# Quarter sums of the MLP's second weight: from accumulating transfers to VectorE, and another order of the mixed products behind them

## The chip, the cores and the metric

The kernel runs on one core of a Trainium2 chip. The metric is the device time of one execution in microseconds (us). A core has five instruction streams that matter here: TensorE (PE), VectorE (DVE), ScalarE (ACT), GpSimd (POOL) and SyncE (SP). Each works through its own stream in order. In this kernel POOL and SP issue transfers and do no arithmetic; a transfer is named here by the queue that issues it.

## What is computed

One layer of a decoder on a sequence of 2048 rows and 1024 channels, all in fp32:

```python
h = x * (1 + sc1) + sh1
z = h @ w_in                       # 1024 -> 2048: gates B and C, values v (3 x 512), pool (512)
y_conv = B * short_conv(C * v)     # causal, width 3
y_pool = multi_scale_pool(pool)    # windows 2, 4, 8, 16, a 128x128 map per window
x = layer_norm(ALPHA * x + (1 + g1) * (concat(y_conv, y_pool) @ w_out))
h = x * (1 + sc2) + sh2
f = square(relu(h @ w_mlp_in)) @ w_mlp_out        # 1024 -> 4096 -> 1024
x = layer_norm(ALPHA * x + (1 + g2) * f)
```

The shifts, scales and gates come from a conditioning vector c through a linear map.

## The kernel before

**Products.** Every fp32 matrix is held as a high part and a low part (`split`, L80 to L82: ScalarE casts the high part at L81, VectorE subtracts it at L82 and gets the low part). A product is three matmuls, high by high, high by low, low by high (`mm3`, L85 to L88). Large products are done by the Strassen-Winograd scheme, seven half-size products in place of eight, in the order

```python
ORDER = (("11", "11"), ("12", "21"), ("s2", "2"), ("s1", "1"), ("s3", "3"), ("s4", "22"), ("22", "4"))
```

The first name is the left operand (a block, or a sum s1 to s4 of blocks), the second the right one (a block, or a weight sum 1 to 4). "s1 by 1" is the fourth of these, "12 by 21" the second.

**Stages.** The sequence is worked in two blocks of 1024 rows (b = 0 and 1). Each goes through the input projection, the output projection with the first layer norm, the MLP's first product (up) in 8 groups of 512 hidden channels, and its second product (down) with the second layer norm. All buffers are in pools: o (12 tiles of 128x1024), h (28), w (6), r (5), and PSUM (8 banks).

**Input projection of block 1** (`in_proj_1`, L616). Four groups j, interleaved. At the end of a group other than the last, `store_mixed` (L340) sends the group's results and their Strassen sums to `msum` in DRAM by four transfers on POOL's queue; the output projection loads them back as r tiles (r<-msum). In the same queue, behind these stores, stand calls of `sum_quarters`.

**Quarter sums.** In block 1, three of down's seven products are themselves done by the Strassen scheme on quarters of 256 columns. Their right operands are sums of quarters of the weights, `wquart`, for n = 0, 1, 2 (product 12 by 21 is n = 0, s4 by 22 is n = 1, s1 by 1 is n = 2). `sum_quarters(n, step)` (L993) makes them with transfers alone, DRAM to DRAM, 512 KB each: step 0 copies (L1001), steps 1 to 3 add into what was copied (L998). There are 24 copies and 24 accumulating transfers, all on POOL's queue. The table `SUM_TURNS` (L717) puts most of them behind the input projection's groups; three more calls stand in the output projection (L935, L936, L945).

**Output projection** (`out_proj`, L852). `load_x` (L859) loads a tile of 128 rows of x, also on POOL's queue: four tiles ahead of the first product, four ahead of product 3. Products accumulate into four PSUM banks X and four banks Y, which is all eight. `begin` (L877) is a VectorE instruction, ALPHA times x plus a bank, which frees nothing until x is there; `end` (L881) adds a further bank.

**Up** (`up`, L1006). A group is 7 products of 24 matmuls of 128x512. Its results are stored as usum by POOL; in block 1 three of them go as quarters, with their sums, to `uquart` (`save_quarters`, L968). In block 0 the same loop also makes the sums of the weights for down, `w2sum`, by `sum_blocks` (L951): loads of 256 KB on SP, four VectorE adds of 128x512, four stores on POOL, at the end of a group.

**Down of block 1** (`down`, L1116). The first 37 units are mixed by the string `MIX`: a "1" is a unit "c", one group of a whole product (product 0, then product 2: 8 units of 24 matmuls of 128x512 each), a "0" a unit "f", one of the seven quarter products of a product k in the order of `FINE` (1, 5, 3), 48 matmuls of 128x256. An f unit reads uquart and wquart (L1140 to L1145). Its bank is evicted by ScalarE (`fine_copy`, L1173) or VectorE (`fine_add`, `fine_less`, `fine_from`, L1177 to L1185), in pieces of 128x256 into the result tiles F. Product 0 stays in PSUM, and VectorE adds it to F (L1286 to L1288) after the last quarter product of k = 1.

Of the kernel before, what the change touches and what calls it, by code (L numbers as in the profile page):

```python
# [11 lines left out]
ALU = mybir.AluOpType  # L12
# [20 lines left out]
WW = T + HALO  # L33
MIX = "1110101010101000100100100101001001001"

# [8 lines left out]
def tile_hybrid_layer(ctx: ExitStack, tc: tile.TileContext, opening, xT, x, wada, vec, win0, win,  # L44
# [295 lines left out]
    def store_mixed(j, y, pt, u, v):  # L340
        for i, r in ((0, y), (2, pt), (4, u[:, :T])):
            nc.gpsimd.dma_start(msum[i : i + 2, j].rearrange("a p n -> p a n"),
                                r.rearrange("p (a n) -> p a n", a=2))
        return nc.gpsimd.dma_start(msum[6, j], v[:, :H]).ins

# [270 lines left out]
    def in_proj_1(X, W, first_w):  # L616
# [14 lines left out]
        def group(j):  # L631
# [58 lines left out]
            if last:  # L690
                mixed[1] = sums[0]
                mixed.extend(sums[1:])
            else:
                done = store_mixed(j, y, pt, u, v)
            with nullcontext() if last else tc.issue_after(done):
                for n, step in SUM_TURNS[j]:
                    sum_quarters(n, step)

# [15 lines left out]


    SUM_TURNS = (((0, 0),), ((1, 0), (0, 1)), ((2, 0), (1, 1), (0, 2)), ((2, 1), (1, 2), (0, 3)))

# [134 lines left out]
    def out_proj(b, ops):  # L852
# [80 lines left out]
        ops.whole(5)  # L933
        if b:
            sum_quarters(2, 2)  # L935
            sum_quarters(1, 3)  # L936
        matmuls(4, Y, False, every, first_row)
# [5 lines left out]
        back(0)  # L943
        if b:
            sum_quarters(2, 3)  # L945
        matmuls(6, X, False, every, last_row)
# [40 lines left out]

    def quarter_sum(n, hf, i):
        return wquart[n, hf, i].rearrange("p (g n) -> p g n", n=Q)

    SUM_STEPS = (((0, 1), (2, 1), (1, 3), (3, 2)), ((0, 0), (2, 3)), ((1, "0"),), ((3, "1"),))

    def sum_quarters(n, step):  # L993
        for hf in range(2):
            for i, what in SUM_STEPS[step]:
                src = quarter_sum(n, hf, int(what)) if what in ("0", "1") else weight_quarter(n, what, hf)
                if step:
                    nc.gpsimd.dma_start(quarter_sum(n, hf, i), src, accum_op=ALU.add,  # L998
                                        max_dma_last_dim=4096)
                else:  # L1000
                    nc.gpsimd.dma_start(quarter_sum(n, hf, i), src)  # L1001

# [113 lines left out]
    def down(b, F, g2, close):  # L1116
# [3 lines left out]
        if b:  # L1120
            parts_ = [("f", k, m) for k in FINE for m in range(7)]
            groups = [("c", i, g) for i in (0, 2) for g in range(NC)]
# [64 lines left out]
        def fine_product(i, m, ops):  # L1187
            bank = {0: "x", 1: "y", 2: "x", 3: "z", 4: "x", 5: "z", 6: "x"}[m]
            new = m in (0, 1, 3)
            if new:  # L1190
                fine_banks[bank] = t_ps()
            ps = fine_banks[bank]
            fine_matmuls(ps, ops, new)
            how, row, col = {0: (fine_copy, 0, 0), 1: (fine_add, 0, 0), 2: (fine_copy, 0, 1),
                             3: (fine_copy, 1, 1), 4: (fine_less, 1, 1), 5: (fine_from, 0, 1),
# [72 lines left out]
        if b:  # L1268
            table[0] = X, True, lambda t, ps: None
            table[2] = X, False, first_row  # L1270
# [4 lines left out]
        for n, (kind, i, part_) in enumerate(units):  # L1275
# [8 lines left out]
            if kind == "f":  # L1284
                fine_product(i, part_, ops)
                if (i, part_) == (1, 6):  # L1286
                    for t in range(4):
                        add(t, lo_, X[t])  # L1288
                if (i, part_) == (3, 6):
                    for t in range(4):  # L1290
# [105 lines left out]
    def mlp(b, B, back, g2):  # L1396
# [9 lines left out]
        if b == 0:  # L1406
            for g in range(NC):
                sums += [(sum_blocks, w2[g], w2sum[g], p) for p in halves]
                if g == 3:
                    sums += [(sum_weights, wins[0], winsum, p) for p in halves]  # L1410

        for g in range(NC):
            for _ in ups[g]:
                pass
            for make, src, dst, p in sums[: HALF_SUMS[g]]:
                make(src, dst, t_o, which=[p])
            del sums[: HALF_SUMS[g]]
# [71 lines left out]
```

## Time and profile before

| | |
|---|---|
| time, 3 runs | 1799.73, 1800.35, 1802.71 us (median 1800.35) |
| profiled execution | 1806.26 us |
| its span in the trace | 1804.5 us |
| mean granted TensorE clock | 0.984 |
| busy: TensorE, VectorE, ScalarE, POOL | 1735.6, 1330.3, 890.4, 276.5 us |
| moved by transfers | 514.04 MB, 285 GB/s |

How to read it. Busy times are those of one profiled execution, and the span is the time from its first to its last instruction. A row of a window gives its start and end, its length, the busy time of an engine with the count of its instructions, then the clock that TensorE was granted (1.00 is full), the busy share of the DMA engines and what they moved in GB/s. A row of the waits names the waiting engine and line, behind the arrow the engine and line that ended the wait, then the total, the number of waits and the longest. In a row of a timeline the brackets hold the idle time before the instruction and what ended it. L878 is line 878 of the kernel before.

### The profile page before, as it was taken

The page shows a single profiled execution, that of the slowest core. Times are in us where ns is not written, and L with a number is a line of the kernel's source. Part 1 is how long each engine was busy: PE and PEld are TensorE (multiplying, and loading weights), DVE is VectorE, ACT ScalarE, POOL GpSimd, SP SyncE. Part 2 cuts the span into 40 slices and gives each one's busy share as a digit, 9 for nine tenths or more (in the row PEclk, how much of TensorE's full clock was granted, in tenths as well). Part 3 has the DMA queues.
Part 4 walks back from the last instruction along what each step waited for, and adds up shares of the span by engine and source line. Part 5 has one row for each costly group of instructions (what it writes and reads, how often), then busy time and mean ns, then how long its engine had stood idle before and what let it go on. Part 6 is the DMA issues. An engine that isn't in the chain of part 4 may idle for free.

```text
span 1804.5 us, 22616 instructions
## 1 busy us (share of the span) xinstructions
PE 1735.6 (96%) x8132; PEld 1452.8 (81%) x8132; DVE 1330.3 (74%) x1756; ACT 890.4 (49%) x1202; POOL 276.5 (15%) x493
## 2 busy tenths in 40 slices
PE   9999999999999999999999983999999998999997
PEld 7888888888888888888788762788888887899986
DVE  7897788876777866687766762688766766997675
ACT  5322467544456544454743330685454455675552
POOL 0222120232222000001001322102221112100000
PEclk9999999999999999999999986999999999999999
DMA  9899766788878998789645899766554469999884
GB/s 385 324 346 336 293 238 247 292 316 319 332 296 326 417 349 308 278 315 362 223 150 192 264 284 245 230 229 222 210 205 171 154 222 388 419 391 325 292 319 180
DMA packets 158304, 514.04 MB, mean 285 GB/s; under 512 B 18288, under 2 KB 23920, under 8 KB 157936
## 3 DMA queue, kind: packets, MB, share of 16 engines
q1 hardware_dynamic: 102960, 315.97, 48.0%
q0 software_dynamic: 55232, 196.64, 30.6%
q8 instruction: 63, 1.03, 0.2%
q14 instruction: 49, 0.40, 0.1%
HBM read 359.97 MB, written 177.73 MB: 298 GB/s over the span
## 4 chain that ended last, share of the span: by engine, by line
PE 80%; DMA 8%; DVE 5%; issue 4%; ACT 2%; POOL 1%; SPq 0%; DVEq 0%; POOLq 0%; ACTq 0%
PE ps L87 24%; PE ps L86 24%; PE ps L88 23%; PE ps L1163 6%; PE ps L403 3%; DMA wquart<-in_w2q 2%; DVE h L82 1%; DVE o L91 1%; DMA o<-in_x 1%; PE ps L759 1%; DMA r<-msum 1%; DMA r<-in_xT 1%; DVE o L1365 1%; DVE o L1359 1%; ACT h L81 0%
## 5 line engine op out<-in xcount | busy, mean ns | idle before, releaser
L86 PE MATMUL ps<-h,w 128*128 128x512 f32 x1312 | 511.5, 390 | 8.2 <-DVE o L91 3.0
L88 PE MATMUL ps<-h,w 128*128 128x512 f32 x1312 | 511.9, 390 | 2.6 <-DVE w L82 2.6
L87 PE MATMUL ps<-h,w 128*128 128x512 f32 x1312 | 511.5, 390 | 0.0
L86 PE MATMUL ps<-h,h 128*128 128x512 f32 x928 | 364.0, 393 | 36.6 <-DVE o L878 30.7
L81 ACT CAST h<-r 128x1024 fp32r<-128x1024 f32 (+1 forms) x202 | 205.8, 1021 | 339.5 <-PE ps L87 117.2
L87 PE MATMUL ps<-h,h 128*128 128x512 f32 x928 | 363.5, 392 | 0.3 <-DMA h<-wlow 0.2
L88 PE MATMUL ps<-h,h 128*128 128x512 f32 x928 | 363.3, 391 | 0.0
L82 DVE TENSOR_TENSOR h<-r,h 128x1024 fp32r<-128x1024 f32 (+1 forms) x202 | 238.3, 1184 | 130.7 <-ACT h L81 129.8
L81 ACT CAST w<-r 128x1024 fp32r<-128x1024 f32 x156 | 164.3, 1053 | 271.6 <-PE ps L87 260.6
L86 PEld LDWEIGHTS ps<-h,w 128*128 128x128 f32 x1312 | 246.9, 188 | 61.3 <-DVE o L91 3.4
L88 PEld LDWEIGHTS ps<-h,w 128*128 128x128 f32 x1312 | 247.1, 188 | 55.0 <-DVE w L82 3.7
L87 PEld LDWEIGHTS ps<-h,w 128*128 128x128 f32 x1312 | 246.9, 188 | 51.8 <-DVE h L82 0.5
L82 DVE TENSOR_TENSOR w<-r,w 128x1024 fp32r<-128x1024 f32 x156 | 190.6, 1222 | 122.8 <-ACT w L81 121.5
L86 PEld LDWEIGHTS ps<-h,h 128*128 128x128 f32 x928 | 175.6, 189 | 75.4 <-DVE o L878 30.2
L87 PEld LDWEIGHTS ps<-h,h 128*128 128x128 f32 x928 | 175.7, 189 | 36.9 <-DMA h<-wlow 1.2
L88 PEld LDWEIGHTS ps<-h,h 128*128 128x128 f32 x928 | 175.4, 189 | 36.4
L91 DVE TENSOR_TENSOR o<-o,o 128x1024 f32<-128x1024 f32 (+2 forms) x222 | 183.3, 836 | 24.1 <-DMA usum<-o 17.8
L91 DVE TENSOR_TENSOR o<-o,ps 128x512 f32<-128x512 f32 (+1 forms) x168 | 110.2, 663 | 54.4 <-PE ps L88 54.0
L82 DVE TENSOR_TENSOR h<-w,h 128x1024 fp32r<-128x1024 f32 x114 | 138.9, 1218 | 10.4 <-ACT h L81 10.2
L1163 PE MATMUL ps<-h,h 128*128 128x256 f32 x1008 | 125.1, 285 | 7.1 <-ACT h L81 3.7
L1163 PEld LDWEIGHTS ps<-h,h 128*128 128x128 f32 x1008 | 124.2, 194 | 8.7 <-ACT h L81 6.5
L81 ACT CAST h<-w 128x1024 fp32r<-128x1024 f32 x114 | 119.7, 1050 | 17.4 <-DMA w<-w2sum 7.2
(158 smaller groups left out, 1444.8 us busy)
## 6 DMA issues: line engine op xcount, KB each, us to landing
usum<-o POOLq DMA_DIRECT2D x88, 512.0 KB, 3.8
r<-usum SPq DMA_DIRECT2D x88, 512.0 KB, 6.8
w<-w2sum SPq DMA_DIRECT2D x62, 512.0 KB, 7.6
r<-in_w SPq DMA_DIRECT2D x60, 512.0 KB, 5.7
r<-uquart SPq DMA_DIRECT2D x42, 512.0 KB, 6.8
o<-in_w SPq DMA_DIRECT2D x72, 256.0 KB, 6.1
w2sum<-o POOLq DMA_DIRECT2D x64, 256.0 KB, 5.9
w<-in_w SPq DMA_DIRECT2D x32, 512.0 KB, 6.5
```

What stands on the lines that cost most here:

```text
L81: high = nc.scalar.copy(hi, src)
L82: return high.ins, nc.vector.tensor_tensor(lo, src, hi.bitcast(F32), op=ALU.subtract).ins
L86: nc.tensor.matmul(ps, whi, xhi, start=first, stop=False, skip_group_check=goes_on)
L87: nc.tensor.matmul(ps, whi, xlo, start=False, stop=False, skip_group_check=goes_on)
L88: nc.tensor.matmul(ps, wlo, xhi, start=False, stop=last, skip_group_check=goes_on)
L91: return nc.vector.tensor_tensor(out_, a, b_, op=op)
L403: nc.tensor.matmul(ps[m, h], wt[:, w : w + P], A[k][p // 2][:, hs], start=k == 0 and p == 0, stop=k == KD - 1 and p == 2)
L759: nc.tensor.transpose(ps[:, t * P : t * P + P], R[4 * h + t][:, k * P : k * P + P], ident)
L1163: nc.tensor.matmul(ps, a[:, us], w[:, gs], start=not begun, stop=hf == 1 and g == 3 and a is ul, skip_group_check=True)
L1359: nc.vector.scalar_tensor_tensor(z[:, cuts[i]], self.F[t][:, cuts[i]], mv[:, 0:1], self.rows[0][:, cuts[i]], op0=op, op1=ALU.mult)
L1365: nc.vector.scalar_tensor_tensor(z[:, cs], z[:, cs], mv[:, 6:7], self.rows[1][:, cs], op0=ALU.mult, op1=ALU.add)
```

## The change

First, `sum_quarters` and its table go. In their place `begin_quarters(n, hf, part)` issues four loads of 256 KB on SP into two o tiles, and the function that it returns does four VectorE adds of 128x512 and four stores of 256 KB on POOL. The 12 sets stand in the loop of up of block 1, `QUARTER_SUMS` of them a group: the loads ahead of the group's last part in the program, adds and stores behind it. Second, in the mixed part of down `MIX` is another string, and the quarter products run in the order k = 3, 1, 5 (s1 by 1, 12 by 21, s4 by 22). Product 0 is copied to F by ScalarE, and product 12 by 21 is added to F by VectorE in all of its seven parts. The added half of k = 3 is summed after k = 5 in place of after k = 3.

```diff
-MIX = "1110101010101000100100100101001001001"
+MIX = "1111" + "01" * 4 + "0" + "001" * 8
+QUARTER_SUMS = (1, 1, 2, 2, 2, 2, 1, 1)
...
-                done = store_mixed(j, y, pt, u, v)
-            with nullcontext() if last else tc.issue_after(done):
-                for n, step in SUM_TURNS[j]:
-                    sum_quarters(n, step)
+                store_mixed(j, y, pt, u, v)
...
-    SUM_TURNS = (((0, 0),), ((1, 0), (0, 1)), ((2, 0), (1, 1), (0, 2)), ((2, 1), (1, 2), (0, 3)))
...
         ops.whole(5)
-        if b:
-            sum_quarters(2, 2)
-            sum_quarters(1, 3)
         matmuls(4, Y, False, every, first_row)
...
-        if b:
-            sum_quarters(2, 3)
         matmuls(6, X, False, every, last_row)
...
+    def begin_quarters(n, hf, part_):
+        a, b_ = t_o(T), t_o(T)
+        tiles = b_[:, :H], a[:, H:], b_[:, H:], a[:, :H]
+        for i, r in enumerate(tiles):
+            nc.sync.dma_start(r.rearrange("p (g n) -> p g n", n=Q),
+                              weight_quarter(n, i, hf)[:, 2 * part_ : 2 * part_ + 2])
+
+        def finish():
+            b11, b12, b21, b22 = tiles
+            tt(b11, b11, b12, ALU.add)
+            tt(b12, b12, b22, ALU.add)
+            tt(b22, b11, b22, ALU.add)
+            tt(b21, b21, b22, ALU.add)
+            for i, r in enumerate((b11, b22, b12, b21)):
+                nc.gpsimd.dma_start(wquart[n, hf, i][:, halves[part_]], r)
+
+        return finish
...
-            parts_ = [("f", k, m) for k in FINE for m in range(7)]
+            parts_ = [("f", k, m) for k in (3, 1, 5) for m in range(7)]
...
+            if i == 1:
+                how, row, col = {0: (fine_add, 0, 0), 1: (fine_add, 0, 0), 2: (fine_less, 0, 1),
+                                 3: (fine_add, 1, 1), 4: (fine_less, 1, 1), 5: (fine_add, 0, 1),
+                                 6: (fine_add, 1, 0)}[m]
+                how(i, row, col, ps)
+                return
...
         if b:
-            table[0] = X, True, lambda t, ps: None
             table[2] = X, False, first_row
...
-                if (i, part_) == (1, 6):
-                    for t in range(4):
-                        add(t, lo_, X[t])
-                if (i, part_) == (3, 6):
+                if (i, part_) == (5, 6):
                     for t in range(4):
                         tt(F[t][:, hi_], F[t][:, hi_], F[t + 4][:, hi_], ALU.add)
...
+        quarters = [(n, hf, p) for n in (2, 0, 1) for hf in range(2) for p in range(2)] if b else []
         for g in range(NC):
+            begun = [begin_quarters(*quarters.pop(0)) for _ in range(QUARTER_SUMS[g])] if b else []
             for _ in ups[g]:
                 pass
+            for finish in begun:
+                finish()
             for make, src, dst, p in sums[: HALF_SUMS[g]]:
```

Line numbers of the changed kernel differ by a few (L878 is L874 there). In rows of the order of instructions, a name with a number is a tile of that pool, and x with a number at the end counts equal rows.

POOL's queue at the end of block 1's input projection. Before, between the msum stores of the last group that is stored and the loads of x:

```order
L342 DMA msum<-o_8173 128x2x512
L342 DMA msum<-o_7826 128x2x512
L342 DMA msum<-o_7901 128x2x512
L344 DMA msum<-o_7825 128x512
L1001 DMA wquart<-w2sum 512x1x256 x8
L998 DMA wquart<-in_w2q 128x1024 x4
L998 DMA wquart<-wquart 128x1024 x2
L998 DMA wquart<-w2sum 512x1x256 x4
L998 DMA wquart<-wquart 128x1024 x4
L861 DMA o_8444<-in_x 128x1024
L861 DMA o_8446<-in_x 128x1024
L861 DMA o_8448<-in_x 128x1024
```

Now:

```order
L343 DMA msum<-o_8153 128x2x512
L343 DMA msum<-o_7818 128x2x512
L343 DMA msum<-o_7893 128x2x512
L345 DMA msum<-o_7817 128x512
L857 DMA o_8402<-in_x 128x1024
L857 DMA o_8404<-in_x 128x1024
L857 DMA o_8406<-in_x 128x1024
L857 DMA o_8408<-in_x 128x1024
```

The 22 transfers of wquart that stood between the stores of msum and the loads of x are out of the queue, and the loads of x follow the last store directly.

VectorE in up of block 1, in the program's order. Before:

```order
L91 TENSOR_TENSOR o_10360<-o_10133 128x256 x2
L91 TENSOR_TENSOR o_10360<-o_10360,o_10133 128x256
L91 TENSOR_TENSOR o_10406<-o_10406,ps_10413 128x512
L91 TENSOR_TENSOR o_10360<-o_10133,o_10360 128x256
L91 TENSOR_TENSOR o_10406<-o_10406,ps_10426 128x512
L82 TENSOR_TENSOR w_10514<-r_10370,w_10513 128x1024
L82 TENSOR_TENSOR w_10547<-r_10369,w_10546 128x1024
L82 TENSOR_TENSOR w_10593<-r_10371,w_10592 128x1024
L91 TENSOR_TENSOR r_10717<-r_10643,r_10644 128x1024
```

Now, where o_10705, o_10706, o_10711 and o_10712 are the tiles of two sets:

```order
L92 TENSOR_TENSOR o_10706<-o_10706,o_10705 128x512
L83 TENSOR_TENSOR w_10863<-r_10719,w_10862 128x1024
L92 TENSOR_TENSOR o_10755<-o_10755,ps_10762 128x512
L92 TENSOR_TENSOR o_10755<-o_10755,ps_10775 128x512
L92 TENSOR_TENSOR o_10705<-o_10705 128x512
L92 TENSOR_TENSOR o_10712<-o_10712,o_10711 128x512
L92 TENSOR_TENSOR o_10705<-o_10706,o_10705 128x512
L92 TENSOR_TENSOR o_10711<-o_10711 128x512
L92 TENSOR_TENSOR o_10706<-o_10706,o_10705 128x512
L92 TENSOR_TENSOR o_10711<-o_10712,o_10711 128x512
L92 TENSOR_TENSOR o_10712<-o_10712,o_10711 128x512
L83 TENSOR_TENSOR w_10896<-r_10718,w_10895 128x1024
```

The adds of the sets are woven between the splits of the group's weights (w<-r) and the additions of PSUM banks (o<-o,ps), which are themselves unchanged. In SP's queue the loads of a group's sets stand between the first and the other three weight blocks of a later group.

VectorE in the mixed part of down, where the rows h<-r and h<-w are splits of operands (low parts), o_11460 to o_11463 the first four tiles of F and ps_11540 to ps_11543 the banks of product 0. Before, at the end of the quarter products of k = 1:

```order
L91 TENSOR_TENSOR o_11460<-ps_12018,o_11460 128x256
L91 TENSOR_TENSOR o_11461<-ps_12018,o_11461 128x256
L82 TENSOR_TENSOR h_12316<-r_12311,h_12315 128x1024
L82 TENSOR_TENSOR h_12320<-w_12312,h_12319 128x1024
L82 TENSOR_TENSOR h_12328<-r_12323,h_12327 128x1024
L82 TENSOR_TENSOR h_12332<-w_12324,h_12331 128x1024
L91 TENSOR_TENSOR o_11460<-o_11460,ps_11540 128x512
L91 TENSOR_TENSOR o_11461<-o_11461,ps_11541 128x512
L91 TENSOR_TENSOR o_11462<-o_11462,ps_11542 128x512
L91 TENSOR_TENSOR o_11463<-o_11463,ps_11543 128x512
```

Now, in the quarter products of k = 1 (o_11580 and o_11581 are the first two tiles of F there):

```order
L92 TENSOR_TENSOR o_11580<-o_11580,ps_12569 128x256
L92 TENSOR_TENSOR o_11581<-o_11581,ps_12569 128x256
L83 TENSOR_TENSOR h_12637<-r_12632,h_12636 128x1024
L83 TENSOR_TENSOR h_12641<-w_12633,h_12640 128x1024
L83 TENSOR_TENSOR h_12700<-r_12695,h_12699 128x1024
L83 TENSOR_TENSOR h_12704<-w_12697,h_12703 128x1024
L92 TENSOR_TENSOR o_11580<-o_11580,ps_12644 128x256
L92 TENSOR_TENSOR o_11581<-o_11581,ps_12644 128x256
```

The four adds of 128x512 from the banks of product 0 are gone, and each part of 12 by 21 now has its own pair of adds of 128x256 behind it, between the splits.

More of the change, by code (lines that the diff above doesn't have):

```diff
@@ L343, in store_mixed @@
                                 r.rearrange("p (a n) -> p a n", a=2))
-        return nc.gpsimd.dma_start(msum[6, j], v[:, :H]).ins
+        nc.gpsimd.dma_start(msum[6, j], v[:, :H])
     def first_group(A):
@@ L986, in weight_quarter @@
         return w2sum[4 * hf : 4 * hf + 4, 0, :, i * Q : i * Q + Q].rearrange("g p n -> p g n")
[L988 to L1001, printed above, removed]
+    def begin_quarters(n, hf, part_):
[13 more added lines that the diff above has]
+        return finish
     def sum_out(g, tiles):
```

## The prediction

> **What bounds the kernel now.** The page first: TensorE is busy for 96% of the span, so a change of order can win only from the small rest and from slices in which the clock is low:
>
> ```profile
> PE 1735.6 (96%) x8132; PEld 1452.8 (81%) x8132; DVE 1330.3 (74%) x1756; ACT 890.4 (49%) x1202; POOL 276.5 (15%) x493
> ```
>
> Next the windows of TensorE by stage (start and end, length, busy time, granted clock, DMA share, GB/s): end of the input projection of block 1 and its output projection (1000 to 1200), up (1200 to 1480), the first 120 us of the mixed part of down (1480 to 1600).
>
> ```profile
> 1000.00:1085.00 85.00, 72.89 (x293) 0.92 1.02 292
> 1085.00:1114.00 29.00, 0.00 (x0) 0.59 0.99 205
> 1114.00:1200.00 86.00, 82.29 (x379) 0.96 0.83 270
> 1200.00:1480.00 280.00, 279.38 (x1232) 1.00 0.53 188
> 1480.00:1600.00 120.00, 112.43 (x691) 0.99 1.01 396
> ```
>
> Length less busy time is TensorE's idle time: 12.1 + 29.0 + 3.7 = 44.8 us in 1000 to 1200, 0.6 in up, 7.6 in the part of down. The waits of TensorE say who ended them (total, times, longest), first in 1000 to 1130 and in 1130 to 1200:
>
> ```profile
> PE ps L86 <- DVE o L878: 29.5, 1, 29.5
> PE ps L86 <- DVE o L91: 8.5, 3, 3.3
> PE ps L88 <- DVE w L82: 1.8, 1, 1.8
> PE ps L86 <- ACT o L625: 1.7, 1, 1.7
> PE ps L759 <- DVE o L890: 2.2, 1, 2.2
> PE ps L86 <- DVE o L878: 1.2, 1, 1.2
> ```
>
> And in 1480 to 1560 and from 1560:
>
> ```profile
> PE ps L1163 <- ACT h L81: 3.7, 1, 3.7
> PE ps L1163 <- DVE h L82: 1.1, 1, 1.1
> PE ps L1163 <- DVE o L91: 2.4, 1, 2.4
> ```
>
> The 29.5 us are one wait for L878, the VectorE instruction that adds a finished PSUM bank to a row tile of x; all eight banks are in use there, so the next product can't begin. The timelines show why VectorE is late (POOL's first, then VectorE's row; start, duration, what, idle time before; wquart holds the quarter sums of the weights):
>
> ```profile
> 1078.03 1.15 POOL L998 DMA_DIRECT2D wquart<-w2sum  x1 [8.73 <-issue]
> 1093.70 1.17 POOL L998 DMA_DIRECT2D wquart<-w2sum  x1 [14.53 <-issue]
> 1094.33 3.95 POOL L998 DMA_DIRECT2D wquart<-wquart  x4
> 1096.92 3.00 POOL L861 DMA_DIRECT2D o<-in_x  x3
> ```
>
> ```profile
> 1113.66 0.69 DVE L878 SCALAR_TENSOR_TENSOR o<-o,ps 128x512 f32<-128x512 f32 x1 [30.73 <-DMA o<-in_x]
> ```
>
> VectorE waited 30.7 us for x. The loads of x (L861) stand on POOL's queue behind the accumulating transfers of wquart, one of which was issued at 1078.0 and the next only at 1093.7. Nothing in x is late by itself: the queue is.
>
> **Part 1, sum_quarters leaves POOL's queue.** The 24 copies and 24 accumulates go, and the loads of x follow the msum stores directly. So the long wait goes, with the 1.2 us at L878 that follows it and the low clock behind it. The clock cost is (1 - granted) x busy, by these rows:
>
> ```profile
> 1032.40:1036.00 3.60, 3.58 (x10) 0.59 0.96 331
> 1062.00:1064.60 2.60, 2.47 (x6) 0.63 1.06 318
> 1066.80:1074.00 7.20, 7.20 (x19) 0.58 1.06 253
> 1114.40:1119.00 4.60, 4.60 (x14) 0.69 1.04 424
> 1512.00:1515.00 3.00, 1.84 (x8) 0.70 1.02 414
> ```
>
> The stretch at 1114 costs 0.31 x 4.60 = 1.4 us, so 29.5 + 1.2 + 1.4 = 32.1 us go with the x loads. That part I take whole.
>
> The short stalls before 1085 (8.5 + 1.8 + 1.7 = 12.0 us), with the dips behind them (1.5 + 0.9 + 3.0 = 5.4 us), make 17.4 us more. There VectorE sits in order behind splits (L82) of operands that are loaded late. The transfers of 1000 to 1125, in all and by kind (count, KB each, us to landing):
>
> ```profile
> DMA packets 11040, 34.53 MB, mean 276 GB/s; under 512 B 1088, under 2 KB 3136, under 8 KB 10905
> ...
> wquart<-in_w2q POOLq DMA_DIRECT2D x16, 512.0 KB, 13.7
> wquart<-w2sum POOLq DMA_DIRECT2D x12, 512.0 KB, 20.5
> wquart<-wquart POOLq DMA_DIRECT2D x10, 512.0 KB, 14.7
> ...
> r<-wosum SPq DMA_DIRECT2D x4, 512.0 KB, 20.7
> ```
>
> 38 transfers of wquart at 0.52 MB are 19.9 of 34.5 MB. Without them 14.6 MB in 125 us are 117 GB/s, and the r loads, 20.7 us now, have the DMA engines nearly to themselves. The nearest row without such transfers is the output projection of block 0, the same code, at a higher rate than these 117 GB/s:
>
> ```profile
> 260.00:330.00 70.00, 70.00 (x333) 1.00 0.70 248
> ```
>
> It has no idle time at all. So of the 17.4 us the ends are 0 (late for a reason of their own) and 17.4; nearest is block 0, but its operands come from another input projection, and I take 13. Part 1 is 32 + 13 = **-45 us**, between -32 and -49.5.
>
> The Trainium skill ("TensorE: Matmul & The Clock Gate", Part 1, the clock gate) has the clock halve only after an idle window of about 3.4 us. By that rule the three dips before 1085 wouldn't be owed to waits of at most 3.3 us, would stay, and the sum would be 5.4 us smaller. The rows show 0.58 to 0.63 right behind such waits, and I go by the rows.
>
> **Part 2, the sums on VectorE in up.** 12 sets, 1 or 2 a group, each 4 loads of 256 KB on SP, 4 adds of 128x512, 4 stores on POOL. Block 0 does up to 3 such sets a group in the same loop (for w2sum). Windows of all engines (PE, PEld, DVE, ACT, POOL) for a stretch of block 0 and two of block 1, its adds, and the page's row of its loads:
>
> ```profile
> 402.00:440.00 38.00, 38.00 (x169) 31.46 (x169) 28.76 (x34) 18.45 (x22) 10.13 (x20) 1.00 0.85 318
> 1200.00:1260.00 60.00, 60.00 (x265) 49.38 (x264) 54.50 (x61) 35.80 (x42) 9.72 (x16) 1.00 0.50 185
> 1298.00:1336.00 38.00, 38.00 (x170) 31.45 (x169) 25.83 (x34) 18.53 (x23) 8.26 (x14) 1.00 0.51 184
> L91 DVE TENSOR_TENSOR o<-o,o 128x512 f32<-128x512 f32 x36 | 24.7, 686 | 0.7 <-DMA o<-in_w 0.4
> o<-in_w SPq DMA_DIRECT2D x72, 256.0 KB, 6.1
> ```
>
> Two sets are 8 x 0.686 = 5.5 us of VectorE: 25.8 + 5.5 = 31.3 of 38 us. Their 16 transfers are 4.2 MB in 38 us, so 184 + 110 = 294 GB/s; block 0 ran at 318 with TensorE at 38.00 of 38. The loads are issued a group (38 us) before their adds and land in about 6. The sets' loads queue on SP ahead of a later group's weights, and their stores on POOL ahead of usum's, as w2sum's do in block 0. What covers the 12 x 2.7 = 33 us of VectorE is its idle time. Tight is only 1200 to 1260: 54.5 plus one set's 2.7 to two sets' 5.5 makes 57 to 60 of 60 us. If that runs over, TensorE waits there, by up to about one product (24 of 170 matmuls of 38 us, 5.4 us). Below nothing it can't go, since up has only 0.6 us of idle time to win. I take **+1 us**, ends 0 and +5.
>
> **Part 3, the mixed map of down.** The 3.7 + 1.1 us at 1512 are the first quarter product's operands, saved in up's last group and loaded back. Now the first quarter product is s1 by 1, whose left quarter is saved at least one product earlier in that group (5.4 us), and one more whole unit stands before it (another 5.4): 10.8 us against a wait of 4.8. The 2.4 us are TensorE waiting for VectorE while four 128x512 adds of the first product stand in its queue; they are gone. Against that, 12 by 21 is now evicted by VectorE:
>
> ```profile
> L91 DVE TENSOR_TENSOR o<-o,ps x16: 408/415/676, 1538.5 to 1685.6; 128x256 f32<-128x256 f32 x12, 128x512 f32<-128x512 f32 x4
> ```
>
> 8 copies leave ScalarE; 14 adds of 0.415 (5.8 us) stand where 6 of these and 4 of 0.676 (5.2 us) did. VectorE's sum is level, but TensorE's bank is given back behind whatever else VectorE has queued. The 7.6 us of idle time and 0.30 x 1.84 = 0.55 us of clock make 8.1 to win; the other end is 0. The stage runs at 396 GB/s, so a wait removed may come back as a load that isn't there: I take **-6 us**.
>
> **Sum.** -45 + 1 - 6 = -50 us: the profiled execution (1806.26 us, span 1804.5) would be 1756.3. It stands 5.9 us over the median of the runs shown, 1800.35; the same 50 us off that give **1750 us**. Best case: -49.5 - 8.1 = -57.6, 1743. Worst within the mechanism: -32 + 5 + 0 = -27, 1773.
>
> **Rivals.**
> (B) The short stalls before 1085 stay: operands of the output projection's first products come from the last input group, whatever the DMA load, and then VectorE's order (splits ahead of PSUM adds) is the cause. For it: the waits name L91, L82 and L625, no transfer; against it: loads of 20.7 us. Then -32 + 1 - 6 = -37: 1763.
> (C) Down gives nothing, being bound by its transfers or by VectorE, and two or so of the twelve sets cost: -45 + 0 + 1 to 5 and some loss on the evictions, 1756 to 1767.
> The Trainium skill ("DMA: Bandwidth & Descriptors", Specifications) gives a limit of about 358 GB/s of HBM for a core. By it the 396 x 120 = 47.5 MB of down's first part would take 133 us of its 120, and (C) would be certain for down; the 396 of the row, held for 120 us, speaks against that limit here.
> (D) Slower: the quarter loads land late. Each set's four adds then hold VectorE's in-order queue, the next group's PSUM adds stand behind them, and TensorE loses about a product, 5.4 us, per set: 12 x 5.4 = 65, less the 50, is 1815. It decides from 50 / 12 = 4.2 us a set. Against it: the 36 adds of block 0 idled 0.7 us in all, with loads issued much closer before them.
> (E) x stays late behind the msum stores (they wait for VectorE's sums on the same queue) or the 50 us return elsewhere: 1797 to 1804.
>
> **How the numbers follow.** Forecast 0.66, around 1750 (1743 to 1758); B 0.16; C 0.10; D 0.04; E 0.04. A measurement of this kernel can tell about 0.2%, 3.6 us, from no change. Faster: 0.66 + 0.16 + 0.10 = 0.92; same is E, 0.04; slower is D, 0.04. The range takes in forecast, B, C and the bounds of the unknown costs: 1742 to 1773.
>
> **What would show it.** In the changed profile: the x loads are issued directly behind the last msum store, some 40 us ahead of their use; no TensorE wait of over 3 us for L878's counterpart; the windows of the output projection near full with the clock at 1.00 (B: two or three waits of 2 to 3 us on VectorE left); up at 38 of 38 us with VectorE near 31; no 3.7 us wait at the first quarter product. I am wrong if TensorE waits in up on VectorE's sums, if a load of x still ends a long wait, or if down's idle time is over 8 us.

## The result, and the profile after

The changed kernel takes 1774.57 us (median of 4 runs, 1772.57 to 1775.48), the kernel before 1801.45 beside it: a ratio of 0.985, interval 0.9833 to 0.9867. That is 27 us faster. Forecast were 1750 us and a range up to 1773; the median lies 1.6 us outside it. The profiled execution took 1773.79 us, its span is 1771.9, 32.6 us under that of before.

Where the 32.6 us come from is read by cutting both traces: the end of block 1's input projection, the output projection, up, and down with the end. The first window starts at the same time in both, 929.70; the other cuts are at the same work, the first matmul of the stage. First the windows of before (start and end, length, TensorE busy with its matmuls, granted clock, DMA share, GB/s):

```profile
929.70:1053.23 123.53, 117.02 (x507) 0.99 0.68 218
1053.23:1179.62 126.39, 88.08 (x369) 0.84 0.91 249
1179.62:1489.02 309.40, 308.78 (x1378) 1.00 0.56 200
1489.02:1804.50 315.48, 298.54 (x1777) 0.99 0.87 330
```

The same stages of the changed kernel:

```profile
929.70:1041.20 111.50, 111.50 (x493) 1.00 0.43 149
1041.20:1121.18 79.98, 79.97 (x369) 1.00 0.60 203
1121.18:1455.82 334.64, 316.37 (x1378) 0.98 0.71 263
1455.82:1771.90 316.08, 299.77 (x1777) 0.98 0.86 329
```

| stage | before | after | difference | forecast |
|---|---|---|---|---|
| end of input projection | 123.5 | 111.5 | -12.0 (3.2 of it from work that the change doesn't touch) | |
| output projection | 126.4 | 80.0 | -46.4 | -45 with the row above |
| up | 309.4 | 334.6 | +25.2 | +1 |
| down and end | 315.5 | 316.1 | +0.6 | -6 |
| sum | | | -32.6 | -50 |

At 929.70 the changed kernel is ahead already: it starts at 926.74 the matmul that the kernel before starts at 929.90, and the first transfer of wquart of the kernel before is issued only at 961.8. So 3.2 of the 58.4 us of the first two rows are a difference between two executions of the same code, and not the change's. The other 55.2 us are still more than was forecast: TensorE has no idle time left there and runs at full clock. GpSimd's timeline shows the loads of x right behind the last store of msum, as predicted:

```profile
1023.72 0.58 POOL L345 DMA_DIRECT2D msum<-o  x1
1029.19 0.55 POOL L857 DMA_DIRECT2D o<-in_x  x1 [4.89 <-PE ps L88]
1031.65 0.54 POOL L857 DMA_DIRECT2D o<-in_x  x1 [1.91 <-DMA msum<-o]
```

But up gave 25 us back. TensorE's waits in up of the changed kernel (1121 to 1456), where before there was 0.6 us of idle time:

```profile
PE ps L87 <- DVE o L92: 9.6, 4, 2.6
PE ps L87 <- ACT o L1009: 4.5, 3, 2.0
PE ps L89 <- DVE w L83: 4.2, 3, 2.5
```

Together they make 334.64 - 316.37 = 18.3 us of idle time; the other 7.6 us are the same 1378 matmuls running longer (316.37 against 308.78). The clock shows where most of that is. It was halved three times for 3.41 us, behind waits of 2.46, 2.63 and 2.02 us:

```profile
1242.98:1246.39 3.41, 3.41 (x9) 0.50 0.01 2
1369.27:1372.68 3.41, 3.41 (x9) 0.50 0.01 2
1427.30:1430.71 3.41, 3.41 (x10) 0.50 1.05 395
```

That is 5.1 of the 7.6 us. Behind the other seven waits, two of them of 2.48 and 2.47 us, the granted clock stays at 1.00. And in down (1456 to 1700) new waits stand where the old ones stood:

```profile
PE ps L1157 <- DVE h L83: 4.5, 2, 3.1
PE ps L1157 <- DVE o L92: 2.6, 1, 2.6
```

Why VectorE is late in up is told by its own waits there. Before, it waited 0.6 us for weight blocks (r<-in_w) and there were no quarter loads; now:

```profile
DVE r L92 <- DMA r<-in_w: 24.4, 5, 5.6
DVE o L92 <- DMA o<-in_w2q: 21.8, 14, 3.1
DVE o L92 <- DMA o<-w2sum: 14.0, 5, 5.7
```

36 us of waiting for the loads of the quarters, 24 for weight blocks. One group shows how. SP's timeline: four weight blocks, of which the last, the first block of the group after, is issued at 1255.9, then the eight quarter loads of two sets:

```profile
1224.91 31.30 SPq L500 DMA_DIRECT2D r<-in_w  x4
1256.31 9.14 SPq L983 DMA_DIRECT2D o<-in_w2q  x8
```

And VectorE's timeline, where the additions of these sets (o<-o and o<-o,o of 128x512) are due from 1261.5 on, 5 us after the first of these loads was issued:

```profile
1260.60 0.88 DVE L92 TENSOR_TENSOR o<-o,o 128x256 f32<-128x256 f32 x2
1264.62 0.69 DVE L92 TENSOR_TENSOR o<-o,o 128x512 f32<-128x512 f32 x1 [3.15 <-DMA o<-in_w2q]
1265.23 1.22 DVE L83 TENSOR_TENSOR w<-r,w 128x1024 fp32r<-128x1024 f32 x1
1266.37 1.28 DVE L92 TENSOR_TENSOR o<-o,ps 128x512 f32<-128x512 f32 x2
1268.02 0.69 DVE L92 TENSOR_TENSOR o<-o 128x512 f32<-128x512 f32 x1 [0.37 <-DMA o<-in_w2q]
1270.81 1.29 DVE L92 TENSOR_TENSOR o<-o,o 128x512 f32<-128x512 f32 x2 [2.10 <-DMA o<-in_w2q]
```

VectorE stops 3.2 us at the first addition, and the split (w<-r,w) and the PSUM additions (o<-o,ps) that TensorE needs stand behind it. This is rival D of the prediction, at 25 us for the 12 sets where it was priced at 65.

### The profile page after: what moved, and what is told of

It reads as the page before. It is cut to its first block, busy times and chain, and to the rows that moved or that the text cites. A ratio compares the mean times of both kernels' runs of the same rounds, so it can differ in the third digit from the quotient of the medians.

```text
span 1771.9 us, 22855 instructions
## 1 busy us (share of the span) xinstructions
PE 1733.7 (98%) x8132; PEld 1451.0 (82%) x8132; DVE 1356.9 (77%) x1808; ACT 888.2 (50%) x1198; POOL 267.0 (15%) x493
## 3 DMA queue, kind: packets, MB, share of 16 engines
q8 instruction: 63, 1.03, 0.2%
## 4 chain that ended last, share of the span: by engine, by line
PE 74%; DVE 9%; DMA 8%; issue 5%; ACT 1%; SPq 1%; POOL 1%; DVEq 0%; POOLq 0%; ACTq 0%
PE ps L88 22%; PE ps L89 22%; PE ps L87 22%; PE ps L1157 5%; DVE o L92 3%; PE ps L404 2%; DMA o<-in_w2q 2%; DMA r<-in_w 2%; DVE w L83 1%; DVE h L83 1%; SPq L983 1%; DMA uquart<-o 1%; PE ps L755 1%; DMA o<-w2sum 1%; DMA o<-nsave 1%
## 5 line engine op out<-in xcount | busy, mean ns | idle before, releaser
L92 DVE TENSOR_TENSOR o<-o,o 128x512 f32<-128x512 f32 (+2 forms) x258 | 207.5, 816 | 52.3 <-DMA usum<-o 17.7
```

Of the source, the lines that this page charges most:

```text
L92: return nc.vector.tensor_tensor(out_, a, b_, op=op)
```

## The experiments

Thirteen kernels were run. Times are medians, each beside runs of the kernel before on the same chip (1801.4 to 1801.7 in the different sets). All but e8 are edits of the changed kernel; e6, e9 and e11 give its quarter sums back to transfers. The columns up and down are from one trace each.

| run | time, us | ratio to before, interval | up | down and end |
|---|---|---|---|---|
| before | 1801.45 | | 309.4 | 315.5 |
| the change | 1774.57 | 0.985 (0.9833 to 0.9867) | 334.6 | 316.1 |
| e1 no additions | 1757.90 | 0.9756 (0.9742 to 0.9771) | 316.7 | 317.8 |
| e2 no loads | 1752.94 | 0.9731 (0.9716 to 0.9745) | 311.8 | 318.8 |
| e3 additions held back | 1779.57 | 0.988 (0.9865 to 0.9895) | 343.0 | 318.7 |
| e4 old mixed map | 1772.84 | 0.9835 (0.9818 to 0.9852) | 334.5 | 315.6 |
| e5 loads on ScalarE's queue | 1784.61 | 0.9914 (0.989 to 0.9938) | 340.2 | 316.6 |
| e6 sums by transfers, in up | 1760.14 | 0.977 (0.9753 to 0.9787) | 323.4 | 315.2 |
| e7 residual without VectorE | 1778.35 | 0.987 (0.9855 to 0.9885) | 335.0 | 320.6 |
| e8 before, x on SP's queue | 1796.66 | 0.9976 (0.9965 to 0.9988) | 312.2 | 315.5 |
| e9 e6, spread | 1765.51 | 0.9786 (0.9756 to 0.9816) | 318.9 | 322.1 |
| e10 no residual | 1763.50 | 0.9783 (0.9761 to 0.9806) | 336.0 | 306.9 |
| e11 e9, residual later | 1759.72 | 0.9759 (0.9732 to 0.9786) | 320.9 | 316.9 |
| e12 loads ahead of the block | 1752.23 | 0.973 (0.9714 to 0.9746) | 313.2 | 315.8 |
| e13 small sets | 1776.12 | 0.9859 (0.9843 to 0.9875) | 335.6 | 317.9 |

### What holds up: additions, loads or queue?

**e1**, without the additions:

```diff
         def finish():
             b11, b12, b21, b22 = tiles
-            tt(b11, b11, b12, ALU.add)
-            tt(b12, b12, b22, ALU.add)
-            tt(b22, b11, b22, ALU.add)
-            tt(b21, b21, b22, ALU.add)
```

> Leaves out the 48 additions of the quarter sums on VectorE: the loaded quarters are stored as they are. Loads and stores stay where they are. Three theories of the 25 us that up of block 1 gained (334.6 us from its first matmul to the first of down, 309.4 before). L, late loads: VectorE's in-order queue is held by additions whose loads have not landed, and splits and PSUM additions behind them come late: without the additions up is back near 310, total 1749 to 1754. V, added work: VectorE is simply given 33 us more: also 1749 to 1754. Q, SP's queue: the 48 loads push the weight blocks r back, and VectorE waits for those: up stays at 330 or more, total 1770 to 1776.

**e2**, without the loads:

```diff
-            nc.sync.dma_start(r.rearrange("p (g n) -> p g n", n=Q),
-                              weight_quarter(n, i, hf)[:, 2 * part_ : 2 * part_ + 2])
+            nc.gpsimd.memset(r, 0.5)
```

> Leaves out the 48 loads of the quarters; GpSimd fills the tiles with a constant in their place, additions and stores stay. L (late loads): nothing to wait for, total 1749 to 1754. V (VectorE's added work): unchanged, 1772 to 1777. Q (SP's queue, weight blocks pushed back): SP has its old queue again, 1749 to 1754. Together with the run without additions this tells the three apart: L is fast in both, V only without additions, Q only without loads.

The windows of up, first of e1:

```profile
1123.66:1440.34 316.68, 310.79 (x1378) 1.00 0.74 277
```

And of e2:

```profile
1122.64:1434.41 311.77, 309.40 (x1378) 1.00 0.66 241
```

Without loads, and with all 48 additions on VectorE, up is within 2.4 us of before: the added work (theory V) costs at most that. Without additions 18 of the 25 us are gone, and 7 stay with the loads on SP. So most of the loss is late loads that hold VectorE's queue (L). That the smaller part is SP's queue (Q) is argued, not shown: e1 lies above the range that L gave, and VectorE waits 33.2 us for weight blocks in it, but it waits 18.8 us for them in e2 as well, where up loses next to nothing.

**e3**, the additions later:

```diff
-            for finish in begun:
-                finish()
+            for finish, mark in zip(begun, marks[g]):
+                with tc.issue_after(mark):
+                    finish()
```

Here `marks[g]` are VectorE's last instructions for the group's fifth and sixth product.

> Everything is computed. The additions of a set are held in the program's order until behind VectorE's last instruction of the group's fifth product (first set) or sixth product (second set), some 15 to 25 us later than now; the loads stay in front of the group. L (late loads): the loads have landed by then, up comes down to 310 to 314, total 1750 to 1755. V (added work): the same work in the same stretch, 1772 to 1777. Q (weight blocks pushed back by loads on SP): the loads are still there, 1768 to 1776.

Up became 343.0 us, a miss for every theory. VectorE no longer waits for quarter loads in this trace, but SP now does, for the stores that free the o tiles of the next set (waits of SP in up):

```profile
SPq L983 <- DMA wquart<-o: 61.9, 7, 15.7
```

The weight blocks are behind these loads in SP's queue. Later additions free the tiles later, and the wait has moved from one queue to another.

**e5**, the loads on another queue: `nc.sync` becomes `nc.scalar` in the line that e2 takes out.

> The 48 loads of the quarters are issued by ScalarE's queue instead of SP's; all else as changed. In the last runs up took 311.8 us without the loads, 316.7 without the additions, 343.0 with the additions held back (there the o tiles came free later and SP waited for them with the weight blocks behind it), 334.6 as changed. Theory S: the loads are late because on SP they stand behind a weight block that waits for its r tile, and they hold later weight blocks in turn; on another queue both go: up 312 to 320, total 1751 to 1760. Rival O: they are late because the o tiles come free too late for any queue: up 330 or more, total 1770 to 1780, and worse if ScalarE, waiting for an o tile, holds its evictions.

It is slower, 1784.6. ScalarE's own waits in up show why, at L1009, the eviction of PSUM behind the loads in its queue:

```profile
ACT o L1009 <- DMA o<-in_w2q: 24.1, 3, 11.4
ACT o L1009 <- DMA uquart<-o: 21.1, 4, 8.5
```

A load that waits for its tile now holds evictions. So this run didn't tell whether the loads were late on SP because of the block ahead of them or because of their tiles, although it spoke for the tiles. Two more runs were made to tell these apart.

**e12**, the order on SP turned round: the first weight block of the group after is queued behind a group's quarter loads.

```diff
-        for i, r in enumerate((a11, a12, a21, a22)):
-            nc.sync.dma_start(r, src[i])
+        ahead = quarter_loads[-2] if up and len(quarter_loads) > 1 else None
+        for i, r in enumerate((a11, a12, a21, a22)):
+            with tc.issue_after(ahead) if ahead and i == 0 else nullcontext():
+                nc.sync.dma_start(r, src[i])
```

> The changed kernel with the order of SP's queue turned round in one place: a group's quarter loads stand ahead of the first weight block of the group after, and that block behind them (now the block stands first, waits some 30 us for its r tile, and the eight loads follow it within 10 us of their additions). The additions keep their place in VectorE's queue. Theory S: that wait is what makes the loads late: up 313 to 320 of 334.6, total 1753 to 1760. Rival O: their o tiles come free no sooner (SP waits at the loads themselves for stores of wquart and uquart): up 328 or more, total 1768 or more.

**e13**, half sets in one o tile:

```diff
-        a, b_ = t_o(T), t_o(T)
-        tiles = b_[:, :H], a[:, H:], b_[:, H:], a[:, :H]
+        a = t_o(T)
+        tiles = [a[:, i * Q : i * Q + Q] for i in range(4)]
...
-QUARTER_SUMS = (1, 1, 2, 2, 2, 2, 1, 1)
+QUARTER_SUMS = (3, 3, 3, 3, 3, 3, 3, 3)
```

> The changed kernel with sets of half the size: 24 sets of 4 loads of 128 KB into one o tile, 4 additions of 128x256, 4 stores, three sets in every group, so that three o tiles are held at a time and not four. SP's order of blocks and loads stays. Theory O (the o tiles are what is short): loads come sooner, up 315 to 325, total 1755 to 1765. Theory S (the wait for an r tile ahead of them in SP's queue): up 328 or more, total 1768 or more.

e12 gives 1752.23 us and up 313.2, e13 nothing (1776.12, up 335.6). SP's timeline of e12: the quarter loads go out from 1228.6 on and the blocks from 1247.6:

```profile
1211.51 15.23 SPq L504 DMA_DIRECT2D r<-in_w  x4
1228.57 4.42 SPq L989 DMA_DIRECT2D o<-in_w2q  x8
1247.61 15.73 SPq L504 DMA_DIRECT2D r<-in_w  x4
```

And VectorE's timeline of e12 at the same additions (o<-o and o<-o,o of 128x512), of which none waits for a load:

```profile
1255.77 1.28 DVE L92 TENSOR_TENSOR o<-o,ps 128x512 f32<-128x512 f32 x2
1256.96 0.69 DVE L92 TENSOR_TENSOR o<-o 128x512 f32<-128x512 f32 x1
1257.57 1.29 DVE L92 TENSOR_TENSOR o<-o,o 128x512 f32<-128x512 f32 x2
```

The first addition starts at 1253.1 there, so the loads have 24 us where they had 5. They still wait for the stores that free their tiles, 18.3 us in all over up, but soon enough. In the changed kernel itself SP waited little for tiles at its quarter loads (its waits in up):

```profile
SPq L983 <- DMA uquart<-o: 4.4, 5, 1.3
```

So the place behind a block that waits for its own tile was the cause (S), and e12 is faster than both kernels, than the change by 22 us.

### The mixed part of down

**e4**, the sums on VectorE with the old map: MIX, the order 1, 5, 3 and product 0 in PSUM as before.

> The sums on VectorE with the mixed part of down as it was before (old string, old order of the quarter products, product 0 left in PSUM). Theory N (the new map moves its waits and wins nothing: down took 316.1 us now and 315.5 before): 1773 to 1776, the same as the whole change. Rival G (the new map wins its 6 us but something else in down eats it, such as the later start of the prefetch): the old map would then be slower still, 1779 to 1782.

1772.84 us, down 315.6: the new map by itself moves its waits and changes nothing that can be told.

**e7**, the residual without VectorE's instructions:

```diff
+            if not b:
                 with tc.issue_after(after[1]):
                     nc.vector.scalar_tensor_tensor(r, r, ALPHA, ag, op0=ALU.mult, op1=ALU.mult)
                 nc.vector.scalar_tensor_tensor(r, ab, ALPHA, r, op0=ALU.mult, op1=ALU.add)
```

> The changed kernel without the 16 VectorE instructions of 1.2 us that scale the residual rows in the mixed part of down (their transfers stay; the output lacks that scaling). Theory T1: the waits of 1.4, 3.1 and 2.6 us that took the place of the old ones in down are VectorE's, which is busy without a gap there; with 19 us less to do they go, with the low clock behind them: down 306 to 309 of 316.1, total 1765 to 1768. Theory T2: the loads at 418 GB/s are the bound; splits wait for them all the same: 1772 to 1776.

**e10**, without the residual at all: the loads of nsave and the stores of rsave go under the same `if not b`.

> The changed kernel without the residual rows in the mixed part of down: neither their 16 transfers of 512 KB nor their 16 VectorE instructions (the output takes older rows in their place). Without the VectorE instructions alone down took 320.6 us against 316.1. Theory T2 (that stretch is bound by its loads, at 418 GB/s; 8.4 MB less are 20 us of transfers): the waits at the fine products go, down 305 to 309, total 1763 to 1768. Rival E (the order of evictions and splits on ScalarE and VectorE is the bound, not the bytes): down stays at 314 to 321, total 1773 to 1779.

The windows of down, first of e7:

```profile
1455.79:1776.40 320.61, 300.68 (x1777) 0.98 0.86 324
```

And of e10:

```profile
1455.98:1762.90 306.92, 296.12 (x1777) 0.99 0.83 311
```

Taking 19 us of work off VectorE did not shorten down (the waits named ScalarE's evictions then, 6.9 us, and it was 4.5 us longer; the total, 1778.35 us, is above the range of either theory); taking the transfers off as well made it 9.2 us shorter than the change, 306.9. Where a run doesn't touch down it took 315 to 322 us, so a few us more say little, but no other run came under 315. So it isn't VectorE's work, although the waits name VectorE: it went with the transfers. ScalarE's waits say the same. From 1490 to 1570 its casts of operands (h) waited 11.2 us for loads of r<-uquart in the changed kernel, and 1.0 us in e10, where these loads landed in 6.0 us (median) and not 10.0. That the bytes bind is the reading that fits; no run takes the bytes alone, since e10 also frees the o tiles and the places in GpSimd's queue that the residual held. The windows of the changed kernel in that stretch:

```profile
1500.00:1520.00 20.00, 18.61 (x127) 1.00 1.03 417
1520.00:1540.00 20.00, 16.92 (x112) 0.91 1.01 381
1540.00:1560.00 20.00, 17.45 (x112) 0.91 1.03 418
```

And of e10, where the transfers are as dense but suffice:

```profile
1480.00:1500.00 20.00, 20.00 (x127) 1.00 1.03 418
1500.00:1520.00 20.00, 20.00 (x135) 1.00 1.01 394
1520.00:1540.00 20.00, 20.00 (x158) 1.00 1.02 396
```

Why down differs by up to 7 us between runs with the same instructions in it (e6 and e9) isn't settled.

### The transfers around the output projection

**e8**, the kernel before with the loads of x of block 1 on SP's queue:

```diff
-            nc.gpsimd.dma_start(xt, x[b * T + len(R) * P : b * T + len(R) * P + P, :])
+            (nc.sync if b else nc.gpsimd).dma_start(xt, x[b * T + len(R) * P : b * T + len(R) * P + P, :])
```

> The kernel before with one edit: in block 1 the eight loads of x are issued on SP's queue instead of GpSimd's; the accumulating transfers stay. The change as a whole took 12.0 us off the input projection and 46.4 off the output projection. Theory X: the long wait is the place in GpSimd's queue alone, so it and what hangs on it go (32 us) and the short stalls stay: output projection 90 to 96 of 126.4, total 1766 to 1772. Rival R: the load on the transfers is the cause and x comes late on any queue: output projection over 105, total 1780 or more.

Only 5 us faster. The output projection takes 115.2 us; TensorE's long wait became four, and when x's loads were issued and what they took to land is on the tile's view (all of e8):

```profile
PE ps L86 <- DVE o L878: 21.0, 4, 9.5
```

```profile
L861 SPq DMA_DIRECT2D o<-in_x x8: 327/328/577, 1062.8 to 1088.9; - x8
DMA to landing us min/median/max: 17.3/24.7/27.0
```

The same rows of the changed kernel:

```profile
L857 POOL DMA_DIRECT2D o<-in_x x8: 531/531/554, 1029.2 to 1057.0; - x8
DMA to landing us min/median/max: 3.5/4.7/9.0
```

Leaving GpSimd's queue was worth 11 us of the output projection's 46.4; the other 35 stayed (rival R's range). Rival R's reason is shown only in part. The loads of x do take 20 us longer to land beside the quarter sums' transfers; but they are also issued late, the first of them 8 us after the output projection has begun (1054.6) and in the changed kernel 12 us before it (1041.2), since SP issues them behind its loads of r<-wosum. How the 35 us divide between the two isn't shown.

### The sums by transfers, in up

**e6** leaves the sums to transfers, as before the change, and only moves them into up, behind a group's stores:

```diff
+            if b:
+                with tc.issue_after(held[g]):
+                    for n, step in SUM_TURNS[g]:
+                        sum_quarters(n, step)
...
+    SUM_TURNS = (((2, 0),), ((2, 1), (0, 0)), ((2, 2), (0, 1)), ((2, 3), (1, 0)), ((0, 2), (1, 1)), ((0, 3), (1, 2)), ((1, 3),), ())
```

> The quarter sums by transfers alone as before the change (24 copies, 24 accumulating transfers on GpSimd's queue), but in groups 0 to 6 of up, each step behind a group's last stores; the new mixed map as changed. Theory: what up lost came with loads on SP, o tiles and additions; none is left, and up has room for 25 MB in 280 us beside its 188 GB/s: up 309 to 313, out projection 80, total 1748 to 1753. Rival P: an accumulating transfer waits for the one before it, the stores of usum and uquart queue behind it on GpSimd's queue, their o tiles come free late, and VectorE waits: up 320 or more, total 1760 or more.

1760.14 us: 41 under before, without a single addition of the quarter sums on VectorE, but up is 323.4. Rival P holds in part: VectorE's waits in up of e6 name the stores behind these transfers and the weight blocks:

```profile
DVE r L91 <- DMA r<-in_w: 23.6, 5, 7.1
DVE o L91 <- DMA usum<-o: 22.4, 5, 11.9
```

**e9** spreads them: `(((2, 0),), ((2, 1),), ((2, 2), (0, 0)), ((2, 3), (0, 1)), ((0, 2), (1, 0)), ((0, 3), (1, 1)), ((1, 2),), ((1, 3),))`.

> The quarter sums by transfers in up, as in the run before that took 1760.1 us (up 323.4, with waits of 4.3 us at 1226 and 3.4 us at 1260, where 4 accumulating transfers and 8 copies stood in one group), but never more than 10 such transfers a group and no two steps of one product in a group, over all 8 groups. Theory P (a dense group holds GpSimd's queue, the stores of usum behind it land late, and VectorE waits for their o tiles): both waits shrink, up 312 to 318, total 1749 to 1755. Rival B (any load on the transfers in up delays the weight blocks r): the waits move to other groups, up 321 to 325, total 1758 to 1762.

**e11** moves the residual on top of e9, from `i == 0 and part_ in (3, 4, 5, 6)` to `i == 2 and part_ in (0, 2, 3, 5)`.

> Everything is computed: the sums by transfers spread over the 8 groups of up, and the residual rows of down moved from the last units of product 0 to units 0, 2, 3 and 5 of product 2, where the mixed part moves 330 GB/s and not 420. Theory T2: down 305 to 310, and with up at 312 to 318 the total is 1739 to 1748. Rival: the residual's transfers collide there with the quarter loads of two fine units in a row, down stays at 314 to 317: the total is that of the spread sums alone.

In e9 up came down by only 4.5 us, with a wait of 4.2 us left at 1230, and the total, above both ranges, isn't told apart from e6 (the intervals overlap). In e11 the waits among the quarter products shrank to one of 2.4 us, but one of 7.4 us came at a later whole product (on VectorE's L91), and down is 316.9: the rival. These three are inconclusive on where the best place is; none beats e12.

## Why the prediction was wrong, point by point

**The step that failed is Part 2**, "The loads are issued a group (38 us) before their adds and land in about 6", and with it the +1 us (0 to 5). They land in 8.0 us (median of those issued from 1256 to 1299), which is near enough; but in the group shown they were issued 5 us before their additions. The text of the program has the loads ahead of a group's products and the additions behind them. The order of the instructions has not: the additions are moved forward to close behind the loads (the rows of VectorE's order stand between the splits of the same stretch), and on SP a weight block for the group after stands ahead of the loads. I saw in the order that the loads lie between a first block and the other three, and priced only what that does to the blocks. What it does to the loads was to be read in the trace of before, from SP's own waits in up (1200 to 1480), where the weight blocks wait for their r tiles:

```profile
SPq L499 <- DVE o L91: 147.4, 12, 23.5
```

Twelve waits, up to 23.5 us, on the queue on which I put loads "a group ahead". e12 shows that this is the whole of it but 3 to 4 us.

**The covering row was of another kind.** Block 0 does three sets a group with no wait, and that is so; but there the loads of two sets were issued from 407.7 on (trace of the changed kernel), ahead of the next group's first block at 430.2, and their additions began at 428.4: 20 us ahead. The same work in another order on the queue isn't the same row.

**Rival D** had the mechanism and its place, with a chance of 0.04, argued down by that same row of block 0. Its price, a whole product of 5.4 us a set, was too high: 25.2 / 12 = 2.1 us a set, of which 1.5 is idle time and 0.6 slower running.

**Part 1** was forecast at -45, between -32 and -49.5, and gave -55.2, without the 3.2 us that were won ahead of it: all of the 44.8 us of idle time went (I had kept 2.2 at L890 and 4.4 of the short stalls with their dips), and 10.4 us of slow running, not 6.8. I had added up four dips in the clock and missed a fifth, 3.41 us at 0.50 from 1165.06 on, behind the 2.2 us at L890. The windows as a whole have it all: 88.08 us for 369 matmuls that now take 79.97, and 2.3 us in the end of the input projection, where the 5.5 us between 117.02 and 111.50 are in part 14 more matmuls (3.2 us). The reason given, "Nothing in x is late by itself: the queue is", said too much: off that queue, in e8, 35 of the output projection's 46.4 us stayed, and the loads of x took 13.8 us to land in the kernel before (median), 24.7 in e8 and 4.7 in the changed kernel. Both the queue and the load on the transfers left with the sums, so the forecast didn't need to tell them apart.

The rule of the Trainium skill ("TensorE: Matmul & The Clock Gate", Part 1, the clock gate), that the clock halves after an idle window of about 3.4 us, had the dips before 1085 stay. They went: the granted clock is 1.00 in both windows, and in up of the changed kernel it halved behind waits of 2.02 to 2.63 us. The rows were right to follow, although seven of the ten waits there have no dip behind them.

**Part 3** was forecast at -6, and down gave +0.6. The named waits went as described (no wait at the first quarter product, none at the additions of product 0), and others of 4.5 + 2.6 us came. That is rival C, and the warning in the text ("a wait removed may come back as a load that isn't there") was the truth of it: e10 with e7 puts it on the residual's transfers and not on VectorE's work. The list of evictions also left out the four copies of product 0 that ScalarE gained (its instructions fell from 1202 to 1198, by 4 and not by 8); no run shows a price for them. I had the return of the waits as the end of the range when the row of 396 GB/s made it the likelier case. The Trainium skill's limit of 358 GB/s for a core ("DMA: Bandwidth & Descriptors", Specifications) isn't where the limit lies here: 417 and 418 GB/s stood for 20 us at a time.

**The sum** by measured terms is -58.4 + 25.2 + 0.6 = -32.6 in the profiled spans (3.2 of it the lead at 929.70), -27 in the medians, since the profiled execution of before stood 4.8 us over its median and that of the change 0.8 under its own. That the miss of the range is as small as 1.6 us is luck: Part 1 gave 10 us more than was forecast and so hid part of what up lost.

## What to carry to other kernels

A load is as early as the place in its queue, not as its place in the program: before a transfer is called hidden, read what stands ahead of it in that queue and how long that waits for a buffer in the trace of before. A wait that names an engine can still be the transfers behind it: take off the work and the transfers one at a time. And where a removed wait leaves a stage at the highest rate that the transfers ever reach, expect the wait back in another place.

## What the runs showed of the hardware that I had not expected

- Short waits can be dearer than they look. In up of the changed kernel ten waits of 0.8 to 2.6 us, 18.3 us in all, came with 7.6 us of slower running in the same 1378 matmuls. The granted clock fell to 0.50 for 3.41 us behind three of them (2.02, 2.46 and 2.63 us) and stayed at 1.00 behind others just as long (2.47 and 2.48 us).
- A load of 512 KB took 24.7 us to land (median of the eight loads of x in e8) beside the accumulating transfers, and 4.7 us in the changed kernel without them. In e8 the stretch of 1000 to 1125 moved 293 GB/s at a DMA share of 1.05, where down of the changed kernel moved 418 GB/s at 1.03: equally busy engines, three tenths fewer bytes.
